# A hybrid pooling / state-space layer in fp32r pieces: the turned stretches of weight products re-chosen, skip weights and last decays taken off the tensor engine, six Silu

## The chip, the cores and the metric

The kernel runs on one core of one Trainium2 chip. The metric is the device time of one execution in microseconds (us), median of several runs. One profiled execution supplies the trace from which every duration below is read. Engines: PE is the tensor engine, DVE the vector engine, ACT the scalar engine, POOL the GpSimd, SP the engine that issues most DMAs.

## The reference

One layer of a streaming encoder, for 256 new positions of one stream (prompt) and 32 of another (sample), 288 columns together, in fp32. D_MODEL is 2048.

```
xn   = rmsnorm(x, norm_mix_pre)
u, z, xbc, dt_raw = split(xn @ w_in)              # 1024 | 2048 | 2560 | 32 columns
y_pool = pool_mixer(u, w_pool) * pool_scale       # trailing means over 2/4/8/16 positions
xbc  = silu(causal_conv4(xbc) + conv_b);  xs, B, C = split(xbc)
dt   = softplus(dt_raw + dt_bias);  A = -exp(a_log)
y, h = ssd_scan(xs, dt, A, B, C, h0) + D * xs     # D = ssd_d, one skip weight per head of 64 channels
                                                  # new h = exp(acum_last) * h0 + states
y_ssd = grouped_rmsnorm(y * silu(z)) * ssd_norm
x    = x + rmsnorm(concat[y_pool, y_ssd] @ w_out, norm_mix_post)
up   = causal_conv3(rmsnorm(x, norm_ffn_pre) @ w_up)   # 2 x 5632 columns
x    = x + rmsnorm((silu(gate) * val) @ w_down, norm_ffn_post)
```

Outputs are x for both streams and the new histories and states.

## The kernel before

**Products in three pieces.** All big products go through `project` (L160). It takes groups of weight columns, most of them 256 wide (two output tiles of 128, `acc` in PSUM), and runs over the contraction in tiles of 128 ("k"). `fetch_w` (L128) loads 8 k-tiles by 256 columns (1 MB) on SP's queue; `split_w` (L143, L144) cuts them into pieces of 4 k-tiles: ACT writes the rounded high part `whi`, DVE the remainder `wlo`. The right side (`xn`, `mixs`, `mixp`, `hn`, `fa`, each 128x288) has been split into high and low in the same way. `mm3` (L150) then issues three matmuls for each k and output tile: `whi` with the high part, `whi` with the low part, `wlo` with the high part. One piece of weights therefore feeds 24 matmuls, 12 for one output tile and 12 for the other. I call such a piece a part, and the 12 matmuls of one output tile in it a block.

**The turned stretches.** `mm3` has an argument `other` that swaps the second and third product: `whi` high, `wlo` high, `whi` low. In the kernel before, the calls of `project` are counted, and in the calls whose number is in `TURNED` (23 numbers) the first part is issued so. Calls 1 to 8 are the convolved xs columns (about 47 to 156 us), 9 to 16 the gate z, 17 to 19 the pooling columns u, 20 to 25 the output product (309 to about 474 us), 26 and on the up and down products.

**Between the products.** The chip's instruction order is set when the kernel is built: a scheduler orders each engine's list by priorities and dependences, except where `pin` or `follow` keep program order. Small matmuls stand between blocks on PE: at 106 us three transposes of per-head rows (`ptok`, L546), two fp32 matmuls that spread per-head numbers over partitions (L554, L555), and the six `pcb` matmuls (L576 to L578); from 125 us on eight groups of 32 `py` matmuls (L646 to L652), one for each four heads; at 280 us a sum over tokens (`psum_t`, L705); at 370 us and later the new states (`pst`, L987, L988).

**Skip weights and last decays.** The skip weight D of each head has to stand on the 64 partitions of that head's channels, the decay exp(acum_last) of each head in every partition. DVE makes two selections of the identity matrix (`sel`, `pick`, `sel64`, L401 to L403), scales one with D (L551) and the identity with `elast` (L552), PE multiplies them out (L554, L555), and DVE copies the result to `dcol` (L562). L659 reads the skip columns of `dcol`, L975 the decay columns.

**Convolution and Silu.** `conv_in` copies a finished output tile into `ebuf`. `conv_out` (L426) makes the first tap on ACT (L432), three taps on DVE (L434), a tanh on ACT (L438), and two products on DVE (L439 for 256 columns, L440 for 32) that complete the Silu. It is called for 16 xs tiles and 4 B/C tiles.

**The scan.** DVE forms the cumulated decays `g` (L519 to L526). SP stores them (`g_d`, L528), POOL loads four heads' rows over all partitions (`gb`, L592), ACT turns them into masks `m` (`ce` L596, L628, exp L631), DVE multiplies them by C·B (L633), and PE uses them in `py`.

Of the kernel before, what the change touches and what calls it, by code (L numbers as in the profile page):

```python
# [8 lines left out]
F32 = mybir.dt.float32  # L9
F32R = mybir.dt.float32r  # L10
AF = mybir.ActivationFunctionType
ALU = mybir.AluOpType
AX = mybir.AxisListType
# [33 lines left out]
COLS = (  # L47
    ("hist_c", 3 * NXC), ("g_mix_post", KD), ("g_ffn_pre", KD), ("g_ffn_post", KD), ("conv_w", 4 * NXC),
    ("conv_b", NXC), ("p_scale", NU), ("ssd_norm", NX), ("hist_u", 15 * NU), ("f_w", 3 * 2 * NF),
    ("f_b", 2 * NF), ("hist_f", 2 * 2 * NF),  # L50
)
SUMS_AT = 11
TURN_AT = 13
FC_GAP = 48
NEAR = 8
W_GAP = 16
TURNED = (1, 6, 7, 8, 9, 11, 13, 14, 16, 17, 19, 20, 21, 23, 26, 27, 28, 30, 40, 46, 54, 65, 76)


@with_exitstack  # L60
def body(
# [95 lines left out]
    def project(view, groups, acts, ksplit, before=None, done=None, spare=(), hold=(), behind=None, wait=(), tail=()):  # L157


        n_all = sum(-(-w // P) for _, w in groups)  # L160
        accs = [acc_ps.tile([P, NT], F32, tag="acc", name="acc") for m in range(n_all - len(spare))]
        accs.extend(spare)
        k_first, k_last = ksplit[0][0], ksplit[-1][0] + ksplit[-1][1] - 1
        groups_done[0] += 1
        turned = groups_done[0] in TURNED
        after = before(*ksplit[0]) if before else None
        for i, (kb, n) in enumerate(ksplit):
            raws = [fetch_w(view, kb, n, c0, w) for c0, w in groups]
            nxt = None
            if before and i + 1 < len(ksplit):  # L170
                nxt = before(*ksplit[i + 1])
            m0 = 0
            for raw, (c0, w) in zip(raws, groups):
                parts = split_w(raw, kb, n, w, tuple(wait) + ((after or ()) if m0 else ()) + (hold if i else tail if m0 + w // P == n_all else ()))
                for q, part in enumerate(parts):
                    for m in range(w // P):
                        c = slice(m * P, (m + 1) * P)
                        with ExitStack() as order:
                            if behind and part[-1][0] == k_last and m0 + m > SUMS_AFTER:
                                order.enter_context(tc.issue_after(behind[-1].ins))  # L180
                            for k, hi, lo in part:
                                mm3(accs[m0 + m], hi[:, c], lo[:, c], acts[k], k == k_first, k == k_last, turned and i + m0 + q == 0)
                        if done and i + 1 == len(ksplit) and q + 1 == len(parts):
                            done(m0 + m, accs[m0 + m])
                m0 += w // P
            after = nxt
        return accs
# [13 lines left out]
    up_ = upool.enter_context(tc.tile_pool(name="upool", bufs=1))  # L201
    start = ExitStack()
    xin = start.enter_context(tc.tile_pool(name="xin", bufs=1))
    busy = xin.tile([P, NT], F32R, name="busy")
    pin(dve.memset(busy.bitcast(F32), 1.0))
    win = w_in
    O_Z, O_X = D_POOL, D_POOL + D_SSD
# [33 lines left out]
    hp = side1.tile([HEADS, 3], F32, name="hp")  # L241
    pin(sp.dma_start(out=hp, in_=heads_in))
    col = {}
    for name, n in COLS:
# [19 lines left out]
    pool.memset(scan_one, 1.0)  # L264
    for c in range(0, NT, 64):
        pool.memset(scan_one[:, c : c + 1], 0.0)
    id32 = ident[:HEADS, :HEADS]

    NE = 4
    ebuf = [const.tile([P, 326], F32, name=f"ebuf{i}") for i in range(NE)]  # L270
# [5 lines left out]
    first += [acc_ps.tile([P, NT], F32, tag="acc", name="acc") for _ in range(5)]  # L276

    for _ in range(BUSY):
        pin(pe.matmul(first[1], busy[:, 0:P], busy, start=True, stop=True))
    last_split = []  # L280
    lows = []
    sq2 = xin.tile([P, 2 * NT], F32, name="sq2")
# [1 line left out]
    def prepare(i):  # L284

        kb, n = CHUNKS[i]
        raw = raws.pop(0)

        w_ = xin.tile([P, 2 * n * NB + W_GAP], F32R, tag="w", bufs=3, name="w")
# [14 lines left out]

        if i:
            for t in tiles:
                high(t)
            for c in PIECES if i < 4 else (slice(0, NB),):
                pin(act.activation(hi[:, :, c], raw[:, :, c], AF.Copy))
# [79 lines left out]
    act.activation(pah, cols[:, c0 : c0 + 5 * NXC], AF.Copy, scale=0.5)  # L389
    g_ssd = side2.tile([P, NX], F32, name="g_ssd")  # L390
    act.activation(g_ssd, col["ssd_norm"], AF.Copy, scale=0.5)
    start.close()


    mixer = ExitStack()
    mp = mixer.enter_context(tc.tile_pool(name="mixer", bufs=1))
    sel = mp.tile([HEADS, 2], F32, name="sel")
    pick = mp.tile([HEADS, NX], F32, name="pick")
    sel64 = mp.tile([HEADS, 2, 64], F32, name="sel64")
    with tc.issue_after(last_split[1].ins):  # L400
        dve.tensor_reduce(sel, id32.rearrange("h (t r) -> h r t", r=2), axis=AX.X, op=ALU.add)  # L401
        dve.tensor_reduce(pick, id32.rearrange("h (t r) -> h t r", r=2), axis=AX.X, op=ALU.add)
        dve.tensor_copy(sel64, sel.unsqueeze(2).broadcast_to([HEADS, 2, 64]))  # L403
    ones_r = const.tile([P, P], F32R, name="ones_r")
    pin(act.activation(ones_r, ones, AF.Copy))
    sc_stage = const.tile([P, 2, 3, NXC], F32, name="sc_stage")
# [19 lines left out]
    def conv_out(i, e, out):  # L426
# [6 lines left out]
        for r in range(1, 4):  # L433
            dve.scalar_tensor_tensor(  # L434
                c, e[:, r : r + 291], cw[:, r, i : i + 1], c, op0=ALU.mult, op1=ALU.add
            )
        th = mp.tile([P, 291], F32, tag="tanh", bufs=2, name="tanh")
        act.activation(th, c, AF.Tanh)  # L438
        dve.scalar_tensor_tensor(out[:, :NP_], th[:, :NP_], 1.0, c[:, :NP_], op0=ALU.add, op1=ALU.mult)  # L439
# [100 lines left out]

    tok = mp.tile([P, 3, 2, HEADS], F32, name="tok")
    tokd = const.tile([P, 3, HEADS], F32, name="tokd")
    p_t = aux([P, 10 * HEADS + NX], "ptok")
    p_tok = p_t[:, : 9 * HEADS].rearrange("p (b h) -> p b h", b=3)
    for b, go in enumerate((0, 256, MW - P)):
        follow(pe.transpose(p_tok[:, b, :], turned[:, go : go + P], ident[: 3 * HEADS, : 3 * HEADS]))  # L546

    hv = htile("hv", NX + HEADS)
    elast = htile("elast", 1)
    act.activation(elast, g[:, 415:416], AF.Exp)  # L550
    dve.tensor_scalar(hv[:, 0:NX], pick, hp[:, 2:3], None, op0=ALU.mult)  # L551
    dve.tensor_scalar(hv[:, NX:], id32, elast, None, op0=ALU.mult)  # L552
    p_ = p_t[:, 9 * HEADS :]
    follow(pe.matmul(p_[:, :NX], sel64.rearrange("h r q -> h (r q)"), hv[:, :NX], start=True, stop=True))  # L554
    follow(pe.matmul(p_[:, NX:], ones[:HEADS, :], hv[:, NX:], start=True, stop=True))  # L555
    dve.tensor_copy(tok, p_tok[:, :, : 2 * HEADS].rearrange("p b (r h) -> p b r h", r=2))
    dve.tensor_copy(tokd, p_tok[:, :, 2 * HEADS :])
    wq = side2.tile([P, HEADS], F32, name="wq")
    for j in range(3):
        dve.tensor_copy(wq[NS * j : NS * (j + 1)], p_tok[P - NS :, 2, 2 * HEADS :])  # L560
    dcol = const.tile([P, NX + HEADS], F32, name="dcol")
    dve.tensor_copy(dcol, p_)  # L562


    bc = []
# [44 lines left out]
    def ssd_quad(q):  # L610
# [45 lines left out]
            ssd_first(q + 1)  # L656
        for i in range(2):
            t = 2 * q + i
            dve.scalar_tensor_tensor(xs[t], xs[t], dcol[:, t : t + 1], ys[i], op0=ALU.mult, op1=ALU.add)  # L659

    def token_sums(p_, sq, first_, last_, pin=False):

# [247 lines left out]
        x1.append(o)  # L910


    bt_h, bt_l = (op_.tile([P, 2, 2, P], F32R, name=n) for n in ("bt_h", "bt_l"))
    bt_s = bpool.tile([P, NT], F32R, tag="b", name="bt_s")[:, : 2 * P].rearrange("p (g c) -> p g c", g=2)
    raw_b = op_.tile([P, 2, NT], F32, tag="du", bufs=6, name="raw_b")
# [50 lines left out]
    def history(g):  # L966

        for i in range(2):
# [389 lines left out]
def _laid_out(v, np):  # L1358
# [6 lines left out]
    def groups(a):  # L1365
# [7 lines left out]
    cols = [  # L1373
        v["state_ssd_conv"], v["norm_mix_post"], v["norm_ffn_pre"], v["norm_ffn_post"], v["ssd_conv_w"],
        v["ssd_conv_b"], v["pool_scale"], v["ssd_norm"], v["cache_pool"], v["ffn_conv_w"], v["ffn_conv_b"],
        v["state_ffn_conv"],
    ]
    return {
        "x_g": np.concatenate([on_partitions(v["norm_mix_pre"]), x], axis=1),
# [4 lines left out]
        "heads": np.stack([v[n][0] for n in ("ssd_dt_bias", "ssd_a_log", "ssd_d")], axis=1),  # L1384
# [32 lines left out]
```

## Time and profile before

| what | value |
|---|---|
| time, median of 3 runs | 1309.49 us (1308.48 to 1309.61) |
| time of the profiled execution | 1309.4 us |
| its span in the trace | 1307.7 us, so 1.7 us lie around it |
| PE busy | 1299.8 us, 10043 matmuls |
| DVE, ACT, POOL busy | 894.3, 672.1, 246.8 us |
| moved by DMA | 251.75 MB, mean 193 GB/s |

PE's busy time is that of pipelined matmuls whose ends are modelled, so it also holds small gaps between them; the pace of PE is better read from the starts of matmuls. A row of the timeline groups neighbours with the same names: "x2" are two matmuls in a row with the same kind of weights.

### The profile page before, as it was taken

What the parts mean: (1) busy time and instruction counts of PE and PEld (TensorE: products, weight loads), DVE (VectorE), ACT (ScalarE), POOL (GpSimd) and SP (SyncE); (2) the same over time, 40 slices, a digit from 0 to 9 for tenths busy, and PEclk for the clock granted to TensorE, in tenths of its full rate; (3) what the DMA queues carried; (4) which work ended last, traced back from release to release, by engine and by line L of the source; (5) the groups of instructions that cost most, each with busy time, mean ns of one, the idle gap of its engine ahead of it and who ended that gap; (6) DMA issues with size and microseconds to landing.
All of it is one profiled execution on the core that took longest, in us unless ns stands there. A gap on an engine that the chain in (4) does not pass through costs nothing.

```text
span 1307.7 us, 25268 instructions
## 1 busy us (share of the span) xinstructions
PE 1299.8 (99%) x10043; PEld 1289.0 (99%) x10043; DVE 894.3 (68%) x1515; ACT 672.1 (51%) x1013; POOL 246.8 (19%) x399
## 2 busy tenths in 40 slices
PE   9999999999999999999999999999999999999998
PEld 9999999999999999999999999999999999999997
DVE  7999988879645588876766643345666676755454
ACT  7557767446543467544444443334444444444442
POOL 2343222222222221211211100001111111201110
PEclk9999999999999999999999999999999999999999
DMA  8668875445576468766554454455544555466663
GB/s 340 191 216 279 288 220 179 161 154 205 208 218 211 153 195 260 215 187 185 172 177 162 155 176 165 162 182 170 184 163 161 172 174 171 162 230 189 214 181 113
DMA packets 110038, 251.75 MB, mean 193 GB/s; under 512 B 64736, under 2 KB 73856, under 8 KB 87392
## 3 DMA queue, kind: packets, MB, share of 16 engines
q1 hardware_dynamic: 103424, 233.22, 54.6%
q0 software_dynamic: 5824, 16.13, 4.2%
q8 instruction: 78, 1.28, 0.4%
q10 hardware_dynamic: 672, 0.80, 0.2%
q14 instruction: 40, 0.33, 0.1%
HBM read 237.11 MB, written 13.00 MB: 191 GB/s over the span
## 4 chain that ended last, share of the span: by engine, by line
PE 96%; issue 2%; DMA 1%; ACT 0%; POOL 0%; DVE 0%; ACTq 0%; POOLq 0%
PE acc L153 89%; PE acc L374 2%; PE acc_x L374 1%; PE acc_x L153 1%; PE py L646 1%; DMA mg<-in_x_g 1%; PE acc L1278 0%; DMA xg<-in_x_g 0%; PE acc L1279 0%; PE py L648 0%; PE acc_t L1301 0%; POOL ho L1006 0%; ACT whi L143 0%; PE acc L381 0%; PE py L652 0%
## 5 line engine op out<-in xcount | busy, mean ns | idle before, releaser
L144 DVE TENSOR_TENSOR wlo<-raw,whi 128x1024 fp32r<-128x1024 f32 (+1 forms) x396 | 473.0, 1196 | 305.6 <-ACT whi L143 304.9
L143 ACT ACTIVATE whi<-raw 128x1024 fp32r<-128x1024 f32 (+1 forms) x396 | 408.3, 1033 | 461.0 <-PE acc L153 367.2
L153 PE MATMUL acc<-hn,whi 128*128 128x288 f32 x2752 | 539.1, 294 | 0.5 <-ACT hn L1054 0.4
L153 PEld LDWEIGHTS acc<-hn,whi 128*128 128x128 f32 x2752 | 436.6, 188 | 1.5 <-ACT hn L1054 0.9
L153 PE MATMUL acc<-hn,wlo 128*128 128x288 f32 x1376 | 400.2, 292 | 0.0
L153 PEld LDWEIGHTS acc<-hn,wlo 128*128 128x128 f32 x1376 | 259.1, 188 | 0.0
L153 PE MATMUL acc<-fa,whi 128*128 128x288 f32 x1320 | 257.6, 294 | 0.0
L153 PE MATMUL acc<-xn,whi 128*128 128x288 f32 x1216 | 239.6, 295 | 0.0
L153 PEld LDWEIGHTS acc<-fa,whi 128*128 128x128 f32 x1320 | 209.1, 188 | 0.0
L153 PEld LDWEIGHTS acc<-xn,whi 128*128 128x128 f32 x1216 | 193.4, 188 | 0.7 <-issue 0.5
L153 PE MATMUL acc<-fa,wlo 128*128 128x288 f32 x660 | 192.4, 292 | 0.0
L153 PE MATMUL acc<-xn,wlo 128*128 128x288 f32 x608 | 178.1, 293 | 0.0
L153 PEld LDWEIGHTS acc<-fa,wlo 128*128 128x128 f32 x660 | 124.4, 188 | 0.0
L1104 POOL COPY fc_stage<-ebuf 128x4 f32<-128x4 f32 x88 | 27.0, 307 | 473.2 <-DVE ebuf L1103 452.0
L153 PEld LDWEIGHTS acc<-xn,wlo 128*128 128x128 f32 x608 | 114.5, 188 | 0.1
L153 PE MATMUL acc<-mixs,whi 128*128 128x288 f32 x512 | 100.9, 294 | 0.0
L1110 DVE SCALAR_TENSOR_TENSOR fc<-ebuf,cols,fc 128x290 f32<-128x290 f32 x176 | 90.2, 518 | 3.6 <-ACT fc L1108 1.0
L1108 ACT ACTIVATE fc<-ebuf,cols 128x290 f32<-128x290 f32 x88 | 54.4, 623 | 73.3 <-DVE ebuf L1103 73.2
L1099 POOL COPY ebuf<-cols 128x2 f32<-128x2 f32 x88 | 69.0, 784 | 109.0 <-DVE fc L1110 94.8
L153 PEld LDWEIGHTS acc<-mixs,whi 128*128 128x128 f32 x512 | 81.5, 188 | 0.1
L153 PE MATMUL acc<-mixs,wlo 128*128 128x288 f32 x256 | 74.4, 294 | 0.0
L153 PE MATMUL acc<-mixp,whi 128*128 128x288 f32 x256 | 50.6, 294 | 0.0
(322 smaller groups left out, 1240.5 us busy)
## 6 DMA issues: line engine op xcount, KB each, us to landing
raw<-in_w_up SPq DMA_DIRECT2D x80, 1024.0 KB, 5.1
raw<-in_w_in SPq DMA_DIRECT2D x38, 1024.0 KB, 5.3
raw<-in_w_down SPq DMA_DIRECT2D x32, 1024.0 KB, 4.9
raw<-in_w_out SPq DMA_DIRECT2D x24, 1024.0 KB, 5.0
raw<-in_w_down SPq DMA_DIRECT2D x16, 768.0 KB, 4.3
raw<-in_w_up SPq DMA_DIRECT2D x14, 512.0 KB, 4.4
gb<-g_d POOLq DMA_DIRECT2D x8, 832.0 KB, 5.9
raw<-in_w_first SPq DMA_DIRECT2D x5, 768.0 KB, 11.9
```

What stands on the lines that cost most here:

```text
L143: act.activation(hi, raw[:, k : k + n, :], AF.Copy)
L144: dve.tensor_tensor(lo, raw[:, k : k + n, :], hi.bitcast(F32), op=ALU.subtract)
L153: pe.matmul(out, w, a[:, x, :], start=start and n == 0, stop=stop and n == 2)
L374: pin(pe.matmul(first[m], w[r][:, k, m * P : (m + 1) * P], xn[kb + k][:, x, :], start=kb + k + r + x == 0, stop=kb + k == KD - 1 and r == 1,))
L646: ins = pe.matmul(y[c, 0:256], xw[:, 0, f_], m[:, h, 0:256], start=True, stop=False)
L1099: pool.tensor_copy(e[:, 258:260], hist_f[:, :, i])
L1104: pool.tensor_copy(fc_stage[:, :, :, i], e[:, 256:324].rearrange("p (s c) -> p s c", c=34)[:, :, 0:2])
L1108: act.activation(c, e[:, 0:290], AF.Identity, bias=col["f_b"][:, i : i + 1], scale=f_w[:, 0, i : i + 1])
L1110: dve.scalar_tensor_tensor(c, e[:, r_ : r_ + 290], f_w[:, r_, i : i + 1], c, op0=ALU.mult, op1=ALU.add)
```

## The change

Four edits.

1. `TURNED` becomes a table from the number of a call of `project` to the number of the part in it that is turned: 16 entries instead of 23, and the part is no longer always the first. Calls 1, 7, 8, 13, 16, 20, 27, 28, 46 and 65 stay in the list, some at another part; 6, 9, 11, 14, 17, 19, 21, 23, 26, 30, 40, 54 and 76 leave it; 5, 10, 12, 15, 18 and 22 are new.
2. The skip weights are repeated on the host into 16 more columns of `cols` (896 columns instead of 880) and used from there. `elast` is stored to DRAM (`e_d`) and loaded back over all partitions (`kept`). The selections, `hv`, `dcol` and the matmuls of L554 and L555 go.
3. Six convolved xs tiles (0 to 5) get two Silu activations on ACT (256 and 32 columns), each with a scale of 2, in place of the tanh and the two DVE products.
4. The matmuls that keep PE busy before the first weights arrive (12 of them, L279) are 256 columns wide instead of 288, and the first weight tiles get 16 more columns of room.

```diff
-TURNED = (1, 6, 7, 8, 9, 11, 13, 14, 16, 17, 19, 20, 21, 23, 26, 27, 28, 30, 40, 46, 54, 65, 76)
+SILU = range(0, 6)
+W_ROOM = 32
+TURNED = {
+    1: 0, 5: 3, 7: 2, 8: 1, 10: 1, 12: 1, 13: 1, 15: 1, 16: 1, 18: 1, 20: 8, 22: 0, 27: 0, 28: 1, 46: 0, 65: 0,
+}
...
-        turned = groups_done[0] in TURNED
+        turned = TURNED.get(groups_done[0])
+        n_part = 0
...
-                                mm3(accs[m0 + m], hi[:, c], lo[:, c], acts[k], k == k_first, k == k_last, turned and i + m0 + q == 0)
+                                mm3(accs[m0 + m], hi[:, c], lo[:, c], acts[k], k == k_first, k == k_last, n_part == turned)
...
+                    n_part += 1
...
-    busy = xin.tile([P, NT], F32R, name="busy")
+    busy = xin.tile([P, 2 * P], F32R, name="busy")
...
-    pin(pe.matmul(first[1], busy[:, 0:P], busy, start=True, stop=True))
+    pin(pe.matmul(first[1][:, : 2 * P], busy[:, 0:P], busy, start=True, stop=True))
...
+    skip = col["skip"]
...
-    with tc.issue_after(last_split[1].ins):
-        dve.tensor_reduce(sel, id32.rearrange("h (t r) -> h r t", r=2), axis=AX.X, op=ALU.add)
-        dve.tensor_reduce(pick, id32.rearrange("h (t r) -> h t r", r=2), axis=AX.X, op=ALU.add)
-        dve.tensor_copy(sel64, sel.unsqueeze(2).broadcast_to([HEADS, 2, 64]))
...
+        if i in SILU:
+            act.activation(out[:, :NP_], c[:, :NP_], AF.Silu, scale=2.0)
+            act.activation(out[:, NP_:], c[:, 259:], AF.Silu, scale=2.0)
+            return
         th = mp.tile([P, 291], F32, tag="tanh", bufs=2, name="tanh")
         act.activation(th, c, AF.Tanh)
...
-    hv = htile("hv", NX + HEADS)
     elast = htile("elast", 1)
     act.activation(elast, g[:, 415:416], AF.Exp)
-    dve.tensor_scalar(hv[:, 0:NX], pick, hp[:, 2:3], None, op0=ALU.mult)
-    dve.tensor_scalar(hv[:, NX:], id32, elast, None, op0=ALU.mult)
-    p_ = p_t[:, 9 * HEADS :]
-    follow(pe.matmul(p_[:, :NX], sel64.rearrange("h r q -> h (r q)"), hv[:, :NX], start=True, stop=True))
-    follow(pe.matmul(p_[:, NX:], ones[:HEADS, :], hv[:, NX:], start=True, stop=True))
+    e_d = dram.tile([HEADS, 1], F32, name="e_d")
+    sp.dma_start(out=e_d, in_=elast)
...
-    dcol = const.tile([P, NX + HEADS], F32, name="dcol")
-    dve.tensor_copy(dcol, p_)
...
-            dve.scalar_tensor_tensor(xs[t], xs[t], dcol[:, t : t + 1], ys[i], op0=ALU.mult, op1=ALU.add)
+            dve.scalar_tensor_tensor(xs[t], xs[t], skip[:, t : t + 1], ys[i], op0=ALU.mult, op1=ALU.add)
...
+    kept = const.tile([P, HEADS], F32, name="kept")
+    sp.dma_start(out=kept, in_=e_d.rearrange("h o -> o h").broadcast_to([P, HEADS]))
...
-            w = dcol[:, NX:][:, heads]
+            w = kept[:, heads]
```

How the instructions stand, at three places. First PE around 106 us, before the change: transposes (`ptok`, L546), the two groups of fp32 matmuls, then `pcb`, and the weights product goes on with a `wlo` product in the middle of a part.

```order
325 L546 MATMUL ptok<-ident,g 128x96 x3
326 L554 MATMUL ptok<-hv,sel_649 128x16
327 L555 MATMUL ptok<-hv,ones 128x32
328 L576 MATMUL pcb<-bc 128x256
329 L577 MATMUL pcb<-bc 128x128
330 L578 MATMUL pcb<-bc 128x32
331 L576 MATMUL pcb<-bc 128x256
332 L577 MATMUL pcb<-bc 128x128
333 L578 MATMUL pcb<-bc 128x32
334 L153 MATMUL acc<-xn,wlo 128x288
335 L153 MATMUL acc<-xn,whi 128x288 x2
```

The same place on PE after the change (line numbers of the changed kernel):

```order
330 L548 MATMUL ptok<-ident,g 128x96 x3
331 L572 MATMUL pcb<-bc 128x256
332 L573 MATMUL pcb<-bc 128x128
333 L574 MATMUL pcb<-bc 128x32
334 L572 MATMUL pcb<-bc 128x256
335 L573 MATMUL pcb<-bc 128x128
336 L574 MATMUL pcb<-bc 128x32
337 L156 MATMUL acc<-xn,whi 128x288
338 L156 MATMUL acc<-xn,wlo 128x288
339 L156 MATMUL acc<-xn,whi 128x288 x2
340 L156 MATMUL acc<-xn,wlo 128x288
```

The fp32 matmuls of `hv` are gone, and `pcb` now ends where the turned part of call 5 begins: one `whi`, then `wlo`, in place of two `whi`.

Second, PE after the `pst` matmuls of about 370 us, where call 22 begins. Before:

```order
1635 L987 MATMUL pst<-xl,bt_h 128x512
1636 L987 MATMUL pst<-xh,bt_l 128x512
1637 L988 MATMUL pst<-xs,bt_s 128x512
1638 L153 MATMUL acc<-mixs,whi 128x288 x2
1639 L153 MATMUL acc<-mixs,wlo 128x288
1640 L153 MATMUL acc<-mixs,whi 128x288 x2
```

After:

```order
1642 L985 MATMUL pst<-xl,bt_h 128x512
1643 L985 MATMUL pst<-xh,bt_l 128x512
1644 L986 MATMUL pst<-xs,bt_s 128x512
1645 L156 MATMUL acc<-mixs,whi 128x288
1646 L156 MATMUL acc<-mixs,wlo 128x288
1647 L156 MATMUL acc<-mixs,whi 128x288 x2
```

The neighbours are the same; the part after `pst` is turned now.

Third, SP's queue around 100 us, where the xs tiles are stored for the scan. Before (its numbers of `xs_d` count the tensors of its build):

```order
24 L128 DMA raw<-in_w_in 128x2048 x2
25 L195 DMA xs_d_951<-blocks 32x9x32 x8
26 L528 DMA g_d<-g 32x416
27 L128 DMA raw<-in_w_in 128x2048 x2
28 L195 DMA xs_d_952<-blocks 32x9x32 x8
```

After:

```order
30 L200 DMA xs_d_941<-blocks 32x9x32 x4
31 L553 DMA e_d<-elast 32x1
32 L131 DMA raw<-in_w_in 128x2048
33 L530 DMA g_d<-g 32x416
34 L200 DMA xs_d_941<-blocks 32x9x32 x4
35 L910 DMA kept<-e_d 128x32
36 L131 DMA raw<-in_w_in 128x2048
```

The store of the last decays stands one weight load ahead of the store of `g`, and their load back five DMAs behind it, each with a weight load behind it in the same queue.

More of the change, by code (lines that the diff above doesn't have):

```diff
@@ L12 @@
 ALU = mybir.AluOpType
-AX = mybir.AxisListType
 PSUM = bass.MemoryType.PSUM
@@ L49 @@
     ("conv_b", NXC), ("p_scale", NU), ("ssd_norm", NX), ("hist_u", 15 * NU), ("f_w", 3 * 2 * NF),
-    ("f_b", 2 * NF), ("hist_f", 2 * 2 * NF),
+    ("f_b", 2 * NF), ("hist_f", 2 * 2 * NF), ("skip", NX),
 )
@@ L240, in body @@
     pin(sp.dma_start(out=cols, in_=cols_in))
-    hp = side1.tile([HEADS, 3], F32, name="hp")
+    hp = side1.tile([HEADS, 2], F32, name="hp")
     pin(sp.dma_start(out=hp, in_=heads_in))
@@ L266, in body @@
         pool.memset(scan_one[:, c : c + 1], 0.0)
-    id32 = ident[:HEADS, :HEADS]
     NE = 4
@@ L287, in prepare @@
         raw = raws.pop(0)
-        w_ = xin.tile([P, 2 * n * NB + W_GAP], F32R, tag="w", bufs=3, name="w")
+        w_ = xin.tile([P, 2 * n * NB + W_ROOM], F32R, tag="w", bufs=3, name="w")
         hi, lo = (w_[:, c : c + n * NB].rearrange("p (k c) -> p k c", k=n) for c in (0, n * NB + W_GAP))
@@ L396, in body @@
     mp = mixer.enter_context(tc.tile_pool(name="mixer", bufs=1))
-    sel = mp.tile([HEADS, 2], F32, name="sel")
-    pick = mp.tile([HEADS, NX], F32, name="pick")
-    sel64 = mp.tile([HEADS, 2, 64], F32, name="sel64")
-    with tc.issue_after(last_split[1].ins):
-        dve.tensor_reduce(sel, id32.rearrange("h (t r) -> h r t", r=2), axis=AX.X, op=ALU.add)
-        dve.tensor_reduce(pick, id32.rearrange("h (t r) -> h t r", r=2), axis=AX.X, op=ALU.add)
-        dve.tensor_copy(sel64, sel.unsqueeze(2).broadcast_to([HEADS, 2, 64]))
     ones_r = const.tile([P, P], F32R, name="ones_r")
@@ L542, in body @@
     tokd = const.tile([P, 3, HEADS], F32, name="tokd")
-    p_t = aux([P, 10 * HEADS + NX], "ptok")
-    p_tok = p_t[:, : 9 * HEADS].rearrange("p (b h) -> p b h", b=3)
+    p_t = aux([P, 9 * HEADS], "ptok")
+    p_tok = p_t.rearrange("p (b h) -> p b h", b=3)
     for b, go in enumerate((0, 256, MW - P)):
         follow(pe.transpose(p_tok[:, b, :], turned[:, go : go + P], ident[: 3 * HEADS, : 3 * HEADS]))
-    hv = htile("hv", NX + HEADS)
     elast = htile("elast", 1)
     act.activation(elast, g[:, 415:416], AF.Exp)
-    dve.tensor_scalar(hv[:, 0:NX], pick, hp[:, 2:3], None, op0=ALU.mult)
-    dve.tensor_scalar(hv[:, NX:], id32, elast, None, op0=ALU.mult)
-    p_ = p_t[:, 9 * HEADS :]
-    follow(pe.matmul(p_[:, :NX], sel64.rearrange("h r q -> h (r q)"), hv[:, :NX], start=True, stop=True))
-    follow(pe.matmul(p_[:, NX:], ones[:HEADS, :], hv[:, NX:], start=True, stop=True))
+    e_d = dram.tile([HEADS, 1], F32, name="e_d")
+    sp.dma_start(out=e_d, in_=elast)
     dve.tensor_copy(tok, p_tok[:, :, : 2 * HEADS].rearrange("p b (r h) -> p b r h", r=2))
@@ L1375, in _laid_out @@
         v["ssd_conv_b"], v["pool_scale"], v["ssd_norm"], v["cache_pool"], v["ffn_conv_w"], v["ffn_conv_b"],
-        v["state_ffn_conv"],
+        v["state_ffn_conv"], np.repeat(v["ssd_d"], 64, axis=1),
     ]
@@ L1383, in _laid_out @@
         "cols": np.concatenate([on_partitions(a) for a in cols], axis=1),
-        "heads": np.stack([v[n][0] for n in ("ssd_dt_bias", "ssd_a_log", "ssd_d")], axis=1),
+        "heads": np.stack([v[n][0] for n in ("ssd_dt_bias", "ssd_a_log")], axis=1),
         "state_nq": v["state_ssd"].reshape(D_SSD, P).T,
```

## The prediction

> **What bounds the kernel now.** I read the page's table of engines first, then PE's waits, then the starts of single matmuls in PE's timeline.
>
> ```profile
> span 1307.7 us, 25268 instructions
> PE 1299.8 (99%) x10043; PEld 1289.0 (99%) x10043; DVE 894.3 (68%) x1515; ACT 672.1 (51%) x1013; POOL 246.8 (19%) x399
> ...
> PE acc L374 <- ACT w L309: 1.1, 1, 1.1
> ...
> PE acc L153 <- ACT hn L1054: 0.4, 1, 0.4
> ```
>
> PE is busy for 99% of the span, and it hardly waits: 1.1 us for the first weights, 0.4 us for `hn`. A change can therefore gain in two ways only: fewer matmuls on PE, or a shorter distance between them. It can lose by making PE wait. So the question is the pace of PE, and the timeline shows two:
>
> ```profile
> 371.31 0.43 PE L153 MATMUL acc<-mixs,whi 128*128 128x288 f32 x2
> ...
> 389.31 0.43 PE L153 MATMUL acc<-mixp,whi 128*128 128x288 f32 x2
> ...
> 400.31 0.42 PE L153 MATMUL acc<-mixs,whi 128*128 128x288 f32 x2
> ...
> 417.86 0.42 PE L153 MATMUL acc<-mixs,whi 128*128 128x288 f32 x2
> ```
>
> Columns are start, duration, engine, line, operation. From 371.31 to 389.31 there are 45 groups of three matmuls (two with `whi`, one with `wlo`): 18.00 us, 0.400 a group, 133.3 ns a matmul. From 400.31 to 417.86 there are 45 groups of the same three: 17.55 us, 0.390 a group, 130.0 ns. Same tiles and sizes, two paces, 0.04 us apart for each block of 12 matmuls. What turns the one into the other? A turned part costs this:
>
> ```profile
> 548.09 0.30 PE L153 MATMUL acc<-hn,whi 128*128 128x288 f32 x1
> ...
> 552.84 0.43 PE L153 MATMUL acc<-hn,whi 128*128 128x288 f32 x2
> ```
>
> At 548.09 begins the turned part of call 30. With the block behind it there are 36 matmuls up to 552.84: 4.75 us, where 36 at 130.0 ns are 4.68. A turned part thus costs 0.07 us where PE was already quick. Now the slow stretches:
>
> ```profile
> 135.70 0.43 PE L153 MATMUL acc<-xn,whi 128*128 128x288 f32 x2
> ...
> 142.10 0.29 PE L153 MATMUL acc<-xn,whi 128*128 128x288 f32 x1
> ...
> 280.45 0.43 PE L153 MATMUL acc<-xn,whi 128*128 128x288 f32 x2
> ...
> 294.85 0.29 PE L153 MATMUL acc<-xn,whi 128*128 128x288 f32 x1
> ...
> 332.89 0.43 PE L153 MATMUL acc<-mixs,whi 128*128 128x288 f32 x2
> ...
> 350.49 0.29 PE L153 MATMUL acc<-mixs,whi 128*128 128x288 f32 x1
> ...
> 390.11 0.29 PE L153 MATMUL acc<-mixs,whi 128*128 128x288 f32 x1
> ...
> 172.93 0.42 PE L153 MATMUL acc<-xn,whi 128*128 128x288 f32 x2
> ...
> 183.46 0.42 PE L153 MATMUL acc<-xn,whi 128*128 128x288 f32 x2
> ```
>
> 135.70 to 142.10 are 16 groups in 6.40 us, 280.45 to 294.85 36 in 14.40, 332.89 to 350.49 44 in 17.60: all 0.400. They begin after `py`, after `psum_t`, within the stretch where pooling products are mixed in, and (371.31) after `pst`. Those at 294.85, 350.49 and 390.11 end with a turned part: "x1" there is one `whi` matmul alone. But 172.93 to 183.46, also after `py`, are 27 groups in 10.53 us, 0.390: there PE came back at the start of a call and not in the middle of a part. My reading: an interruption leaves PE in one of two rhythms, and a turned part brings the quick one.
>
> **The change part by part.** *The table.* Call 7 is turned where the stretch at 135.70 lies: 4 blocks, 0.16 us. Call 18 is turned at part 1, so of the 9 blocks from 280.45 two stay slow: 7 blocks, 0.28. Part 8 of call 20 comes some four blocks after 332.89, of 11: 7 blocks, 0.28. Call 22 is turned directly behind `pst`: 371.31 to 390.11 are 47 groups, 0.47. Together 1.19 us less. Seven turned parts fewer (16 for 23) at 0.07 are 0.49 less; those of calls 30, 40, 54 and 76 lie among the quick `hn` and `fa` products and have nothing to repair. Against that, PE after the first `py` now returns in the middle of a part, with about eight blocks to the turned part of call 7: between 0 and 0.32 us, and nothing tells which, so 0.16. After the third `py` about one and a half blocks are slow: 0.06. Sum −1.19 −0.49 +0.22 = −1.46 us.
>
> [...]
>
> *The fp32 matmuls.* The chain of waits around 106 us:
>
> ```profile
> 106.17 0.32 PE ptok L554 x2
> 106.49 0.24 PE ptok L555 x2
> ```
>
> They stand on PE's path, between matmuls of the same type: 0.32 + 0.24 = 0.56 us less. PE is not left waiting in their place: `pcb` behind them needs only the four B/C tiles, which are convolved first.
>
> *Silu.* Durations by groups (busy us, mean ns):
>
> ```profile
> L438 ACT ACTIVATE tanh<-conv 128x291 f32<-128x291 f32 x20 | 8.7, 437 | 3.5 <-DVE conv L434 3.5
> ...
> L439 DVE SCALAR_TENSOR_TENSOR xs<-tanh,conv 128x256 f32<-128x256 f32 x16 | 6.6, 411 | 0.6 <-ACT tanh L438 0.6
> ...
> L440 DVE SCALAR_TENSOR_TENSOR xs<-tanh,conv 128x32 f32<-128x32 f32 x16 | 2.9, 184 | 0.0
> ...
> L628 ACT ACTIVATE m<-gb,tok 128x32 f32<-128x32 f32 x32 | 9.8, 308 | 0.0
> ...
> L708 ACT ACT_TABLE_LOAD x2 | 2.6, 1283 | 0.0
> ```
>
> DVE loses 6 × (0.411 + 0.184) = 3.57 us. ACT gains at most 0.437 + 0.308 for a tile, for the tanh's 0.437: 6 × 0.308 = 1.85 us, and two more table loads (Silu in, exponential back), 2 × 1.283 = 2.57; 4.4 us in all. Where does that lie?
>
> ```profile
> 60.00:75.00 15.00, 15.00 (x118) 15.00 (x117) 14.97 (x33) 7.28 (x9) 10.43 (x6) 1.00 0.65 196
> 75.00:90.00 15.00, 15.00 (x117) 15.00 (x116) 14.98 (x32) 7.46 (x10) 5.83 (x7) 1.00 0.63 179
> 90.00:105.00 15.00, 15.00 (x118) 15.00 (x117) 14.53 (x40) 8.58 (x15) 4.46 (x10) 1.00 0.73 224
> ```
>
> Columns after the window: length, then PE, PEld, DVE, ACT, POOL busy. DVE is full in all three, ACT half idle, PE unbroken. So the load moves from the full engine to the free one, and ACT has 14 us for 4.4. For PE it is worth nothing, since PE does not wait there: 0. If that cover goes, `whi` would come late by one table load, 1.3 us.
>
> By the Trainium skill ("ScalarE: Activation LUTs", What ACT_TABLE_LOAD costs) a switch of tables costs about 2.66 us with the drain: 5.3 us instead of 2.57 for both, a rule against this edit. Here the load has a row of 1283 ns and no run shows the drain; even 5.3 us would fit the idle time in the windows above.
>
> *The last decays.* Two small DMAs enter SP's queue. `kept` waits for `e_d`, with weight loads behind both; it is used only from 372 us on. But `g_d` stands behind `e_d`, and this is the chain:
>
> ```profile
> 96.66 0.18 ACT L550 ACTIVATE elast<-g 32x1 f32<-32x1 f32 x1
> ...
> 100.20 0.31 SPq L528 DMA_DIRECT2D g_d<-g  x1
> ...
> 101.96 0.72 POOL L606 DMA_DIRECT2D xk<-xs_d  x1 [3.44 <-DMA g_d<-g]
> ...
> 103.94 1.06 POOL L592 DMA_DIRECT2D gb<-g_d  x2
> ...
> DMA to landing us min/median/max: 4.5/5.9/10.0
> ...
> 104.58 0.43 ACT L438 ACTIVATE tanh<-conv 128x291 f32<-128x291 f32 x1
> ...
> 110.48 0.29 ACT L596 ACTIVATE ce<-gb 128x128 f32<-128x128 f32 x1
> ...
> 120.75 1.89 DVE L633 TENSOR_TENSOR m<-m,cbt 128x1664 f32<-128x1664 f32 x1 [1.16 <-ACT m L631]
> ...
> 125.55 0.44 PE L646 MATMUL py<-m,xk 128*64 128x256 f32 x2
> ```
>
> `elast` (96.66) now follows the Silu of the sixth tile and the second table load on ACT. That tile's tanh stands at 104.58; DVE, which feeds it, has about 4.5 us less to do by then (the 3.57 and the selections), the Silu takes 0.3 us more, the load 1.28: about 101.8. With one weight load between, `g_d` goes out near 102.5 instead of 100.20. It takes 101.96 − 100.20 = 1.8 us, so `gb` starts near 104.4 (103.94 before, when POOL had two loads of `xk` ahead of it) and lands near 110.3 by the median, 114.4 by the maximum. From `ce` to the end of the mask on DVE it was 12.2 us (110.48 to 120.75 + 1.89); in the new order the second `ce` and the nine `m` behind it that stood between are moved behind, about 3 us: 9.5 us as an estimate, so the mask ends at about 120. `py` comes 18 matmuls earlier by the order, 2.3 us, and the 0.56: near 122.6 instead of 125.55. Margin 2.6 us by the median: 0. At 10.0 us of landing it is used up, and PE stands 1 to 2 us.
>
> *The start.* 12 matmuls lose 32 columns each:
>
> ```profile
> 1.29 3.25 PE L279 MATMUL acc_x<-busy 128*128 128x288 f32 x12 [1.29 <-DVE busy L205]
> 4.34 2.60 PE L374 MATMUL acc<-xn,w 128*128 128x288 f32 x12
> ```
>
> That shortens 3.05 us by a ninth, 0.3 us, but the matmuls after 4.34 run into the 1.1 us wait of L374 anyway: 0, with bounds of −0.3 (if the data was there) and +0.3 (if the clock comes later).
>
> Sum: −1.46 − 0.56 = −2.0 us on the profiled execution of 1309.4 us: 1307.4 us. The median of the runs, 1309.49, is the same within 0.1 us. About 0.2%, 2.6 us, is what a measurement of this kernel can tell from no change, so the likeliest case is a gain inside that.
>
> **The rivals.**
> 1. *More comes off than the stretches I counted* (chance 0.14). The new order also ends short slow spells (the mixed zone ahead of 332.89, where the gain is not in my sum) and the first 0.3 us. For: PE's rhythm there changes with every interruption. Against: no turned part is placed in that zone. Another 1.2 us: 1306.2.
> 2. *PE falls into the slow rhythm in the long up and down products* (0.09, the slower side). From 548.09 on PE has nothing but these products up to the last call, with turned parts now only in calls 46 and 65. Each 100 us of them at 0.400 in place of 0.390 cost 2.56 us. If the stretch from call 30 to call 46, about 200 us, runs so, that is 5.1 us more: 1312.5. It decides if more than (2.6 + 2.0) / 0.0256 = 180 us run slow. Against: all of it ran at 0.390 before, ahead of the turned parts as well as behind.
> 3. *The order of products is not what sets the rhythm* (0.08). Then only the fp32 matmuls count: 1308.8. For: the blocks after `py` at 172.93 are quick without any turned part.
> 4. *Late masks or splits* (0.15). `gb` lands later than about 112.9 (110.3 plus the margin of 2.6), or a split comes late where DVE is full. PE stands 1 to 4 us; at 2 us 1309.4, at 4.6 us slower by over 0.2%.
>
> **How the numbers follow.** The forecast has 0.54; about 0.14 of it lies beyond −2.6 us, since its open terms (0 to 0.32 after `py`, ±0.3 at the start, a few 0.1 in the mixed zones) reach there. Faster by over 0.2%: 0.14 + 0.14 of rival 1 = 0.28. Slower: 0.09 of rival 2 and 0.07 of rival 4 = 0.16. Within: the rest, 0.56. The range goes from 1305.8 (rival 1 and the start's 0.3) to 1311.4 (rival 4 with 4 us), and leaves out rival 2 and the ends of 1 and 4.
>
> **What would show it.** Right: at call 22, directly after `pst`, groups of 0.390 from the second part on; the same after the second `py` and from part 1 of call 18; no fp32 group between `ptok` and `pcb`; 0.390 at calls 30, 40 and 76 without a turned part. Wrong: slow groups after a turned part; `py` or `acc` rows with idle time released by ACT `m`, DVE `m` or `wlo` between 105 and 160 us; any 0.400 after 530 us.

## The result

The changed kernel takes 1315.55 us (median of 5 runs, 1313.92 to 1315.68) against 1309.03 us for the kernel before (also 5 runs, two more than ahead of the prediction): a ratio of 1.0044, 95% interval 1.0034 to 1.0055. It is slower by some 6 us, where 1307.4 was forecast. The profiled execution has 1314.26 us with a span of 1312.5.

The span and PE's waits, after:

```profile
span 1312.5 us, 25248 instructions
...
PE py L642 <- issue: 2.3, 1, 2.3
...
PE acc L156 <- DVE wlo L147: 0.7, 1, 0.7
...
PE acc L156 <- ACT whi L146: 0.6, 1, 0.6
```

PE now waits 2.3 us ahead of a `py`, 0.7 and 0.6 us for splits; none of the three was there before. Where they lie, and what comes with them, PE's stretches show (length, PE busy with the number of matmuls, granted clock, DMA share, GB/s):

```profile
120.00:122.00 2.00, 1.53 (x12) 1.00 0.50 82
122.00:124.00 2.00, 1.15 (x6) 1.00 0.64 206
124.00:126.00 2.00, 0.71 (x6) 0.85 1.04 384
126.00:128.00 2.00, 1.03 (x6) 0.50 0.85 340
...
130.00:132.00 2.00, 2.00 (x17) 0.50 0.16 34
132.00:134.00 2.00, 2.00 (x16) 0.95 0.94 310
```

PE is idle in pieces from 121 to 127 us, and from about 125.5 to 132 us its clock is granted at half. The chain of work behind this, read back through the timelines of SP, POOL, ACT, DVE and PE:

```profile
101.55 0.31 SPq L553 DMA_DIRECT2D e_d<-elast  x1
101.96 0.37 SPq L131 DMA_DIRECT2D raw<-in_w_in  x1
102.42 0.38 SPq L530 DMA_DIRECT2D g_d<-g  x1
...
111.20 1.06 POOL L588 DMA_DIRECT2D gb<-g_d  x2 [10.83 <-DMA g_d<-g]
...
117.20 0.31 ACT L592 ACTIVATE ce<-gb 128x128 f32<-128x128 f32 x1 [8.95 <-DMA gb<-g_d]
...
124.98 1.88 DVE L629 TENSOR_TENSOR m<-m,cbt 128x1664 f32<-128x1664 f32 x1
...
126.97 1.12 PE L642 MATMUL py<-m,xk 128*64 128x256 f32 x4 [2.26 <-issue]
```

The store of `g` went out at 102.42, as forecast (102.5). It did not land 1.8 us later but at about 110.9, and `gb` was issued at 111.20 where 104.4 was forecast. ACT, which works in order, stood 8.95 us at `ce`, with the splits and masks behind it; PE then ran dry. The row of `py` names no releaser, but it begins 0.1 us after DVE has finished the mask (124.98 + 1.88 = 126.86). While the store was under way the DMA engines moved almost nothing (length, clock, DMA share, GB/s):

```profile
101.00:102.00 1.00, 1.00 0.13 22
...
103.00:104.00 1.00, 1.00 2.97 98
104.00:105.00 1.00, 1.00 0.49 16
...
108.00:109.00 1.00, 1.00 1.02 418
```

So the store did not wait for bandwidth: 16 to 98 GB/s moved from 101 to 108 us, 418 right after. The share of 2.97 comes from packets that last long: the 13 packets of 8 KB that begin between 102.6 and 103.3 us take 4.4 times the 0.7 us of all 16 engines, by this estimate 3.8 us each. In `late_decay` below, which has no `e_d` here, the 13 that begin between 101.0 and 101.5 us take some 1.1 us each.

What the loss adds up to: the rows show 0.6 + 0.7 + 2.3 = 3.6 us of idle time; counted from the start of one matmul to the start of the next, PE loses 4.1 us at these three places. At half clock the `py` group takes from 126.97 to 130.52, 3.55 us, where the same 32 matmuls took 1.89 before, and the first products behind it lose another 0.7; together 2.4 us:

```profile
125.55 0.65 PE L646 MATMUL py<-m,xk 128*64 128x256 f32 x4
...
127.44 0.40 PE L153 MATMUL acc<-xn,wlo 128*128 128x288 f32 x1
```
```profile
130.52 0.61 PE L156 MATMUL acc<-xn,whi 128*128 128x288 f32 x1
```

The first two rows are before the change, the third after it. That is 6.5 us. The span is 1312.5 us against 1307.7, 4.8 more; in `late_decay` below, the changed kernel without this stall, it is 1305.8. So the stall costs 6.7 us of the profiled execution, and the gains elsewhere are worth 1.9.

These gains can be seen. Groups of three in the changed kernel's timeline:

```profile
381.06 0.42 PE L156 MATMUL acc<-mixs,whi 128*128 128x288 f32 x2
...
398.61 0.42 PE L156 MATMUL acc<-mixs,whi 128*128 128x288 f32 x2
...
552.23 0.42 PE L156 MATMUL acc<-hn,whi 128*128 128x288 f32 x2
...
570.17 0.42 PE L156 MATMUL acc<-hn,whi 128*128 128x288 f32 x2
...
132.82 0.43 PE L156 MATMUL acc<-xn,whi 128*128 128x288 f32 x2
...
139.62 0.29 PE L156 MATMUL acc<-xn,whi 128*128 128x288 f32 x1
```

381.06 to 398.61, in call 22 behind `pst`, are 45 groups in 17.55 us: 0.390, where it was 0.400. 552.23 to 570.17, where call 30 was turned before, are 46 in 17.94: 0.390. 132.82 to 139.62, behind the first `py`, are 17 in 6.80: 0.400, the slow end of what I had left open.

### The profile page after: what moved, and what is told of

Same layout as the page of the kernel before. It is cut to its first block, busy times and chain, and to the rows that moved or that the text cites. A ratio compares the mean times of both kernels' runs of the same rounds, so it can differ in the third digit from the quotient of the medians.

```text
span 1312.5 us, 25248 instructions
## 1 busy us (share of the span) xinstructions
PE 1300.5 (99%) x10039; PEld 1288.9 (98%) x10039; DVE 890.6 (68%) x1497; ACT 674.9 (51%) x1021; POOL 249.5 (19%) x399
## 4 chain that ended last, share of the span: by engine, by line
PE 94%; issue 2%; DMA 2%; ACT 1%; POOL 1%; DVE 0%; ACTq 0%; POOLq 0%
PE acc L156 87%; PE acc L378 2%; PE acc_x L378 1%; PE acc_x L156 1%; PE py L642 1%; DMA g_d<-g 1%; PE acc L1276 0%; DMA xg<-in_x_g 0%; DMA gb<-g_d 0%; PE acc L1277 0%; PE acc_t L1299 0%; DMA mg<-in_x_g 0%; PE py L644 0%; POOL msum L720 0%; ACT m L624 0%
```

## The experiments

Theory: the store of `g` lands late because of what stands ahead of it on the DMA side, and all the loss follows from that. Rivals: ACT's own added work makes the masks late; or the store is late because `g` is.

### One part alone, and one weight load moved

`table_alone`: the kernel before with the new `TURNED` and `n_part`.

> The kernel before with the new table of turned parts alone. Rhythm theory: quick groups (0.390 us) directly after pst at 370 us and from part 1 of call 18, slow ones (0.400) shorter by about 1.2 us in sum, seven turned parts fewer at 0.07: about 1.3 us less than before, 1307.7, at the same order around 100 to 130 us. Rival (the order of products does not set the rhythm): within 0.4 us of before, 1309.0.

Measured 1308.06 us, ratio 0.9993 (0.9984 to 1.0002); profiled span 1306.7, 1.0 us shorter. The direction and about the size are those of the rhythm theory; the interval just reaches no change.

`silu_alone`: the kernel before with the six Silu.

```diff
+        if i in range(0, 6):
+            act.activation(out[:, :NP_], c[:, :NP_], AF.Silu, scale=2.0)
+            act.activation(out[:, NP_:], c[:, 259:], AF.Silu, scale=2.0)
+            return
```

> The kernel before with the six Silu alone: no e_d, no kept, old table. On SP's queue a weight load stands directly ahead of the store of g here too. Queue theory: the store of g takes over 5 us, ACT waits for gb, PE is idle near 120 to 127 us and its clock falls; 1312 to 1316. Rival (the two DMAs of the decays, e_d and kept, are what disturbs the queue): no stall, 1308.5 to 1309.5.

Measured 1309.34 us, ratio 1.0000 (0.9991 to 1.0009). SP, POOL and ACT of this run:

```profile
100.60 0.39 SPq L128 DMA_DIRECT2D raw<-in_w_in  x1
101.09 0.38 SPq L532 DMA_DIRECT2D g_d<-g  x1
...
106.63 1.06 POOL L596 DMA_DIRECT2D gb<-g_d  x2 [6.46 <-DMA g_d<-g]
...
113.86 0.31 ACT L600 ACTIVATE ce<-gb 128x128 f32<-128x128 f32 x1 [5.78 <-DMA gb<-g_d]
```

With a weight load directly ahead, the store takes until 106.6, 5.5 us, and ACT stands 5.8 us at `ce`; yet PE does not wait. So a weight load ahead delays the store, but not enough. ACT's added work alone costs nothing that this run resolves.

`kept_alone`: the kernel before with the second edit alone (skip columns, `e_d`, `kept`).

> The kernel before with the skip weights in cols and the decays by e_d and kept alone: no Silu on ACT, old table. On SP's queue e_d stands ahead of the store of g, with three small stores between and no weight load directly ahead. Queue theory: the store of g takes under 4 us, no stall, and the time falls by the 0.56 us of the fp32 matmuls: 1308.4. Rival (e_d and kept disturb the queue): stall as in the changed kernel, 1312 or more.

Measured 1311.22 us, ratio 1.0015 (1.0006 to 1.0024): slower, though the fp32 matmuls are gone and no weight load stands between. From the store of `g` (99.19) to `gb` (103.93) it takes 4.7 us, ACT stands 6.5 us, PE 0.6 us for a `wlo`. My expectation of under 4 us was wrong, and the time lies between the two that I had given: `e_d` or `kept` disturb something by themselves.

`raw_held`: the changed kernel with the weight load between `e_d` and the store of `g` held behind that store.

```diff
...
+            if n_fetch[0] == 14:
+                order.enter_context(tc.issue_after(g_dma[0].ins))
             group, c = divmod(c0, 2 * P)
...
```

> The changed kernel, with the one weight load that stands between the stores of e_d and g on SP's queue held until the store of g is issued; nothing else is edited. Queue theory (the store of g is slow because a 1 MB weight load was issued 0.46 us ahead of it in the same queue): the store lands in 2 to 3 us instead of 8.5, gb starts before 106 us, ACT waits for gb less than 2 us instead of 9.0, PE has no idle time between 120 and 127 us and keeps its clock; the time falls by the 3.6 us of idle and about 2.4 us of half clock, from 1315.5 to about 1309. Rival (ACT's added work, Silu and table loads, makes the masks late whatever the queue does): still idle PE time of 3 us or more and a time of 1313 or more.

Measured 1315.14 us, ratio 1.0046 (1.0033 to 1.0059). The stall stays:

```profile
100.97 0.31 SPq L559 DMA_DIRECT2D e_d<-elast  x1
101.38 0.37 SPq L536 DMA_DIRECT2D g_d<-g  x1
...
107.47 1.06 POOL L594 DMA_DIRECT2D gb<-g_d  x2 [7.72 <-DMA g_d<-g]
...
PE py L648 <- issue: 5.2, 1, 5.2
```

Without the weight load the store still takes 6.1 us, and `gb` then 8.7 to land. My first theory, the weight load as the whole cause, fell with this run; `e_d` and `kept` were left.

### The decays out of the way

`late_decay`: the changed kernel with `e_d` stored behind the load of `h0t` for the sixth four heads, `kept` loaded behind the eighth.

```diff
...
+        if q in (5, 7):
+            with tc.issue_after(h0_dma[q].ins):
+                if q == 5:
+                    sp.dma_start(out=e_d, in_=elast)
+                else:
+                    sp.dma_start(out=kept, in_=e_d.rearrange("h o -> o h").broadcast_to([P, HEADS]))
...
```

> The changed kernel, with the store of the last decays (e_d) moved behind the load of h0t for the sixth four heads and its load back (kept) behind that for the eighth, so that neither stands near the store of g; a weight load still stands directly ahead of that store. Theory A (the tiny store e_d and what follows it in the queue keep the DMA engines from moving data between 101 and 108 us, and so delay g and gb): the store of g takes 5 to 6 us as with Silu alone, gb lands before 113 us, ACT waits for it less than 6 us, PE has under 1 us idle between 120 and 127 us, clock full; 1308 to 1309. Rival B (g itself is late, by Silu and the table load on ACT, and any further delay is enough): idle PE of 3 us, 1313 or more.

`pe_decay`: no `e_d` and no `kept`; the decays through PE as before, the skip weights from `cols`.

```diff
...
-    e_d = dram.tile([HEADS, 1], F32, name="e_d")
-    sp.dma_start(out=e_d, in_=elast)
+    hv = htile("hv", HEADS)
+    dve.tensor_scalar(hv, ident[:HEADS, :HEADS], elast, None, op0=ALU.mult)
+    p_ = p_t[:, 9 * HEADS :]
+    follow(pe.matmul(p_, ones[:HEADS, :], hv, start=True, stop=True))
...
+    dve.tensor_copy(kept, p_)
...
```

> The changed kernel with the last decays spread by the tensor engine as before (one of the two fp32 matmul groups, 0.24 us, back on PE) and no e_d, no kept. Theory A: as with the late store, 0.24 us more: 1308.2 to 1309.3, no stall at py. Rival B: stall, 1313 or more.

`late_held`: `late_decay` with the weight load held behind the store of `g` as well, by the two lines of `raw_held`.

> As with the late e_d and kept, and the weight load ahead of the store of g held behind it too. Both theories of the queue together (a weight load ahead of it and e_d both slow the store of g): the store of g takes 2 to 3 us, gb is issued before 105 us, ACT waits under 3 us for it, PE has no idle time around py; the whole gain of the table and of the fp32 matmuls is left: 1306.5 to 1307.8.

`no_silu`: the changed kernel with tanh throughout.

```diff
-SILU = range(0, 6)
+SILU = ()
```

> The changed kernel with tanh and products for all tiles (no Silu, no added table loads). e_d is issued some 5 us earlier here (as with the decays alone). Theory A: e_d still slows the store of g to 4 or 5 us, ACT waits some 6 us for gb as with the decays alone, PE idle 0.5 to 1 us: 1308.5 to 1310. Rival B (Silu and its table loads are the cause): no wait, 1307.3.

`late_no_silu`: `late_decay` with the same edit.

> The changed kernel with e_d and kept late (as late_decay) and with tanh and products for all tiles, no Silu. If Silu is worth nothing to PE, as the prediction had it: the same as late_decay, 1307.4 within 0.5. If taking 3.6 us from DVE pays, slower than that by 1 us or more; if the table loads cost, faster by 0.5 or more.

| kernel | ahead of the store of g | its issue to that of gb, us | ACT at ce, us | PE idle at py | time, us | ratio (95%) |
|---|---|---|---|---|---|---|
| changed | e_d, weight load | 8.8 | 9.0 | 2.3 | 1315.55 | 1.0044 (1.0034 to 1.0055) |
| late_decay | weight load | 5.2 | 2.3 | 0 | 1307.40 | 0.9987 (0.9979 to 0.9996) |
| pe_decay | weight load | 5.3 | 2.2 | 0 | 1307.34 | 0.9988 (0.9980 to 0.9997) |
| late_held | neither | 2.4 | 2.3 | 0 | 1307.69 | 0.9994 (0.9986 to 1.0002) |
| late_no_silu | neither directly | 2.5 | 3.5 | 0 | 1307.50 | 0.9985 (0.9976 to 0.9994) |
| no_silu | e_d, small stores | 4.7 | 6.4 | 0 | 1308.80 | 0.9998 (0.9989 to 1.0006) |

The store and the load behind it in `late_decay` and `late_held`:

```profile
100.50 0.38 SPq L530 DMA_DIRECT2D g_d<-g  x1
...
105.66 1.06 POOL L589 DMA_DIRECT2D gb<-g_d  x2 [5.58 <-DMA g_d<-g]
```
```profile
100.13 0.32 SPq L536 DMA_DIRECT2D g_d<-g  x1
...
102.57 1.07 POOL L595 DMA_DIRECT2D gb<-g_d  x2 [2.57 <-DMA g_d<-g]
```

Neither ahead: about 2.5 us. A weight load directly ahead: 5.2 to 5.3. With `e_d` as well: 8.8. As soon as `e_d` and `kept` are out of the way the stall is gone and the kernel takes 1307.4 us, the figure that was forecast for the change. That it is the same to the digit is luck: against the kernel before in these runs, 1309.13, it is 1.7 us less, where 2.0 were forecast. Holding the weight load too brings nothing more, since PE no longer waits there. Silu or tanh makes no difference once that is so (1307.40 and 1307.50); with `e_d` in its place, Silu makes it worse. In `no_silu` `e_d` is issued at 96.43, `g` at 98.85, with three small stores and no weight load between; with Silu `elast` comes 5 us later, and `e_d`, the weight load and `g` stand together.

### What about e_d

`kept_late` is `kept_alone` with `kept` loaded behind the last `h0t`:

```diff
...
+        if q == 7:
+            with tc.issue_after(h0_dma[q].ins):
+                sp.dma_start(out=kept, in_=e_d[:, 0:1].rearrange("h o -> o h").broadcast_to([P, HEADS]))
...
```

`e_wide` is `kept_late` with `e_d` stored as 32 rows of 512 B:

```diff
-    elast = htile("elast", 1)
-    act.activation(elast, g[:, 415:416], AF.Exp)
-    e_d = dram.tile([HEADS, 1], F32, name="e_d")
+    elast = htile("elast", P)
+    act.activation(elast, g[:, 415:416].broadcast_to([HEADS, P]), AF.Exp)
+    e_d = dram.tile([HEADS, P], F32, name="e_d")
```

`e_act` is the changed kernel with `kept` late and `e_d` stored from ACT's queue:

```diff
-    sp.dma_start(out=e_d, in_=elast)
+    act.dma_start(out=e_d, in_=elast)
...
```

> The kernel before with the skip weights in cols and the decays by e_d and kept (as kept_alone), but kept loaded behind the last h0t, so that only e_d stands near the store of g. If e_d itself slows the store of g: 4 to 5 us from its issue to the issue of gb, as in kept_alone (4.7). If kept does (it waits at the head of SP's queue): 2 to 2.5 us, as with no e_d (1.8 to 2.4).

> As kept_late, with e_d stored as 32 rows of 512 B (the decay repeated 128 times) in place of 32 rows of 4 B; kept then gathers single values, far from here. If it is the 4-byte pieces that are slow, the store of g takes 2 to 2.5 us again; if any further small store ahead of it counts, 4 to 5 us as in kept_late.

> The changed kernel with e_d stored from ACT's own DMA queue instead of SP's, and kept loaded behind the last h0t. A weight load stands directly ahead of the store of g (worth some 3.5 us). If e_d delays only what stands behind it in its own queue, the store of g takes 5 to 6 us as without e_d (5.2) and PE does not wait: about 1307.5. If its pieces hold up the shared DMA engines, 8 us or more and a stall at py: 1312 or more.

The store of `g` and the issue of `gb` in `kept_late`, then in `e_wide`:

```profile
98.86 1.07 SPq L521 DMA_DIRECT2D g_d<-g  x1
...
103.82 1.06 POOL L580 DMA_DIRECT2D gb<-g_d  x2 [4.08 <-DMA g_d<-g]
```
```profile
98.50 1.23 SPq L521 DMA_DIRECT2D g_d<-g  x1
...
101.43 1.07 POOL L580 DMA_DIRECT2D gb<-g_d  x2 [2.05 <-DMA g_d<-g]
```

5.0 us behind 32 pieces of 4 B, 2.9 us behind 32 pieces of 512 B, in the same place (one run each: 1308.24 and 1308.44 us). The same number of pieces and more bytes, yet less delay. And from another queue:

```profile
100.91 0.37 SPq L530 DMA_DIRECT2D g_d<-g  x1
...
101.73 0.34 ACTq L553 DMA_DIRECT2D e_d<-elast  x1
...
107.59 1.06 POOL L590 DMA_DIRECT2D gb<-g_d  x2 [7.10 <-DMA g_d<-g]
...
116.48 0.31 ACT L597 ACTIVATE ce<-gb 128x128 f32<-128x128 f32 x1 [8.06 <-DMA gb<-g_d]
```

Here `e_d` is issued 0.8 us after the store of `g`, on ACT's queue, and still that store takes 6.7 us (5.2 to 5.5 with no `e_d` near), between the two figures that I had expected. `gb` takes 8.9; in `late_decay` it takes 4.6, but there no weight load is issued just ahead of it, and in `silu_alone`, where one is, it takes 7.2. PE stands 2.2 us at `py`; one run, 1313.06 us. So it seems to be not only the order in SP's queue: the store in 4-byte pieces holds up what other queues have under way. This rests on a single execution. Why the packets beside such pieces last so long no run shows.

The last question was whether this holds in the changed kernel itself, or whether `kept`, waiting at the head of SP's queue, does it there. `changed_kept_late` moves `kept` alone; `changed_e_wide` differs from that in the width of the rows of `e_d` alone.

> The changed kernel with kept loaded behind the last h0t; e_d stays where the change puts it, in 4-byte rows, ahead of a weight load and the store of g. If e_d is what costs: the store of g takes 8 us or more again, ACT waits 8 to 9 us for gb, PE stands at py and its clock falls; 1312 to 1316. If kept at the head of SP's queue is what costs: 5 to 6 us for the store, no stall, 1307 to 1308.

> The same as changed_kept_late in every engine's place around the store of g, with e_d stored as 32 rows of 512 B. If the 4-byte pieces are the cause in the changed kernel: the store of g takes 5 to 6 us (the weight load alone), PE does not stand at py, clock full, 1307 to 1308. If any store there costs: as changed_kept_late, 1312 or more.

SP and POOL of the two, then PE's wait and a stretch behind `py` of the second:

```profile
101.19 0.31 SPq L553 DMA_DIRECT2D e_d<-elast  x1
101.60 0.37 SPq L131 DMA_DIRECT2D raw<-in_w_in  x1
102.06 0.38 SPq L530 DMA_DIRECT2D g_d<-g  x1
...
111.02 1.06 POOL L590 DMA_DIRECT2D gb<-g_d  x2 [11.04 <-DMA g_d<-g]
```
```profile
101.52 0.39 SPq L530 DMA_DIRECT2D g_d<-g  x1
...
106.69 1.06 POOL L590 DMA_DIRECT2D gb<-g_d  x2 [7.34 <-DMA g_d<-g]
...
PE py L647 <- issue: 1.3, 1, 1.3
...
124.00:126.00 2.00, 2.00 (x25) 1.00 0.25 77
```

9.0 us from store to `gb` with 4-byte rows, `kept` far away; 5.2 us with 512-byte rows. The times are 1312.54 us (ratio 1.0027, 1.0016 to 1.0039) and 1308.93 us (0.9999, 0.9988 to 1.0011). It is `e_d`, by the width of its rows; its own store lands after 4.1 us with 4-byte rows and 1.4 with 512-byte rows. With `kept` near as well the time was 1315.55; of these 3 us a part is a longer stretch at half clock (6.8 against 3.4 us, estimated from the granted clock in stretches of 2 us), and what else `kept` does no run shows. In `changed_e_wide` PE still stood 1.3 us and the time is above the 1307 to 1308 that I had expected, but the clock stayed full.

## Why the prediction was wrong

**The failed step** is the one on the last decays: "It takes 101.96 − 100.20 = 1.8 us, so `gb` starts near 104.4". The 1.8 us were measured on a store with no weight load and no `e_d` ahead. The issue of the store was forecast well (102.5, measured 102.42), its duration was carried over to a queue that the change had just altered. It took 8.5 us. I had quoted `e_d` and the weight load that now stood ahead, and priced only the time at which they let the store go out, not what they do to its landing. The step behind it held: from `ce` to the end of the mask it took 9.7 us (117.20 to 126.86) where 9.5 was estimated.

**The rival that came true** is the fourth, late masks or splits, by its own threshold: `gb` was to decide if it landed after 112.9, and it landed at 117.2. Its price was too low: 1 to 4 us of standing PE, measured 4.1 by the starts of matmuls, but the half clock behind the standing was not in it, another 2.4. (The lower end of the range, 1305.8, is 1305.9 by its own terms, 1306.2 − 0.3.) The Trainium skill ("TensorE: Matmul & The Clock Gate", What's actually happening) has the clock halved after an idle window of about 3.4 us. The runs agree in kind: 5.2 us of idle in one piece (`raw_held`) cost the clock, and so did 3.6 us in three pieces here and 0.7 + 2.2 us in `e_act`; 1.3 us in `changed_e_wide` did not.

**The table.** Rightly forecast in its mechanism and in nearly every place: call 22, part 1 of call 18, part 8 of call 20, calls 30 and on. One open term came out at its end: the blocks behind the first `py` were slow throughout (0.17 us from 132.82 alone). Forecast −1.46, `table_alone` −1.05 by the medians, −1.0 by the spans. The spans hold more than the table: call 1 begins at 47.21 us before and at 46.83 in `table_alone`, though nothing ahead of it was changed there, and the stretch behind the output product (about 470 to 516 us) takes 45.2 to 46.2 us in kernels with one and the same table. Between the same matmuls elsewhere `table_alone` is shorter by 0.28 us for call 18 (280.45 to 308.95 before, 280.02 to 308.24), by 0.75 for calls 20 and 22 (308.95 to 421.37, 308.24 to 419.91), whose slow stretches were put at 0.28 + 0.47, and by 0.27 from call 28 on (516.76 to 1166.25, 515.83 to 1165.05), where four turned parts at 0.07 went. These are 1.3 us, close to the forecast.

**The fp32 matmuls and Silu.** The times do not resolve them: `pe_decay`, with one group back on PE, is not slower than `late_decay`. The timelines do: from `ptok` to the product behind `pcb` PE takes 2.67 us before (105.76 to 108.43), 1.95 in the changed kernel (106.79 to 108.74) and 2.46 in `pe_decay` (106.06 to 108.52). So 0.72 us went, where 0.56 was forecast. Silu by itself is worth 0 for PE within what `late_no_silu` and `silu_alone` resolve. The Trainium skill ("ScalarE: Activation LUTs", What ACT_TABLE_LOAD costs) has 2.66 us for a switch of tables with the drain, by estimate 5.3 us for both. This does not show here: in the changed kernel the activation ahead of the load ends at 99.5, the load begins at 99.52 and the next activation 1.29 us later, so no drain is seen on either side.

**The start** was put at 0. The narrower first matmuls were not tried alone; call 1 begins at 47.34 us in the changed kernel, at 47.09 in `late_decay` and 46.97 in `changed_kept_late`, which have the same start, and at 47.21 before: the edit cannot be told from this scatter.

**The sum without the stall** holds: 1307.4 forecast, 1307.40 and 1307.34 measured with the decays elsewhere. These two beat both kernels, by 0.13 and 0.12% in the ratios to the kernel before, and so does `late_no_silu`, by 0.15%. Of the two terms the table gave 1.3 us for 1.46 and the fp32 matmuls 0.72 for 0.56; the two misses cancel.

## What to carry to other kernels

A duration of a transfer belongs to the queue it was measured in: when a change puts other DMAs ahead of or beside a transfer on whose landing an in-order engine waits, price its landing anew, with the nearest row of one that had such neighbours. Judge a store by the width of its pieces, not by its bytes: 32 pieces of 4 B delayed a 52 KB store by about 2 us more than 32 pieces of 512 B did. And when a forecast stall on PE comes to about 3 us, in one piece or in several close together, add the time at half clock behind it.

## What the runs showed of the hardware that I had not expected

- A 128-byte store in 32 pieces of 4 B adds 2.0 us to the store behind it in the same queue (5.0 against 2.9 us with 512-byte rows, 103.82 − 98.86 against 101.43 − 98.50), 3.8 us where a weight load stands there too (9.0 against 5.2), and in one execution about 1.5 us to a store already issued on another queue (6.7 against 5.2). The Trainium skill ("DMA: Bandwidth & Descriptors", Specifications) says that below 512 B the engine reads, modifies and writes; the rows agree that the width counts between 4 and 512 B. Widths between were not tried as such; four stores of `xs_d` in rows of 32 floats (128 B) stand directly ahead of the store of `g` in `late_held` too, and there it takes 2.4 us.
- A 1 MB weight load issued 0.45 us ahead of a 52 KB store doubles its time, from 2.4 us (`late_held`) to 5.2 us (`late_decay`).
- The order of three products on the same tiles moves the pace of fp32r matmuls of 288 columns between 130.0 and 133.3 ns, and a single turned part switches the pace for what follows up to the next interruption: for the 45 groups behind `pst` shown above.
